# P·V of the banded attention with split operands, and a new order table, in a two-layer encoder trunk

## The chip, the cores and the metric

One core of a Trainium2 chip. The metric is the device time of one execution in microseconds (us), less is better. The kernel before takes 986.03 us, the median of three runs (985.98 to 986.37).

## The reference, cut to what matters

Two layers of an encoder on 256 tokens of width 1024. In each, three mixers read the same x (differential attention, a gated delta net in two directions, and attention in a band of 128 tokens to either side), their outputs are merged by gates, projected and normalised; a gated MLP with a short convolution follows. The change touches the third mixer, eight query heads on two key heads of 64:

```python
def window_gqa(q, k, v, sink, bias_table):
    ...
    s = jnp.where(valid[None, :, None, None], s + bias[None, None], -jnp.inf)
    sink_f = sink.astype(jnp.float32).reshape(G, R)[None, None, :, :, None, None]
    m = jnp.maximum(jnp.max(s, axis=-1, keepdims=True), sink_f)
    e = jnp.exp(s - m)
    p = e / (jnp.sum(e, axis=-1, keepdims=True) + jnp.exp(sink_f - m))
    o = jnp.einsum('bngrqk,bnkgd->bnqgrd', p.astype(vw.dtype), vw)
    return o.reshape(B, T, Hq * dh)

def reference(...):
    for l in range(DEPTH):
        h = hybrid_mixer(x, ...)
        x = layer_norm(DEEPNORM_ALPHA * x + h, ln1_g[l], ln1_b[l])
        f = conv_glu_ffn(x, ffn_up[l], ffn_conv[l], ffn_conv_b[l], ffn_down[l])
        x = layer_norm(DEEPNORM_ALPHA * x + f, ln2_g[l], ln2_b[l])
    return x
```

## The kernel before, in words

All arithmetic is float32 or near it. Most matmuls get there by a split: an operand is copied into a rounded type (`F32R`), the part named `hi`, and its remainder is subtracted from the original, `lo`; `mm3` then adds hi·hi, hi·lo and lo·hi, three matmuls of the rounded type. Weights come through SP's queue into `raw` tiles, ACT makes `hi` and DVE makes `lo` (`hi_take`, `lo_take`, and `hi_proj_tok`, `lo_proj_tok` for the projections `wo` and `fd`). Some smaller products are left in plain float32. `A.copy` may go to ACT or to DVE, whichever the plan chooses; `V` is DVE, `TE` is TensorE (PE).

The stages of a layer: products of x with the weights (`mm_proj_ch`, `mm_token_major`), the three mixers, branch products and gates (`mm_product`, labels `wb` and `gz`), the projection `wo` and a norm, eleven FFN chunks c = 0 to 10 (`mm_wide`), and the projection `fd` (`mm_run`, `ch_run`) with the second norm. The first two chunks of the FFN get their second factor from a token-major product (`s_token_major`), transposed on PE.

The program is not issued in the order in which it is written. Every operation is recorded with a cost, then ranked by the longest chain behind it, to which come a term for urgent pieces and the table `PRIO`, which holds a number for the label under which an operation was recorded (`plan.label`, as `(0, 'c', 2)` for layer 0, window attention, t = 2). Operations are placed on the engines by that rank. So one number in the table can move instructions on all engines. Names in `buf("tag")` draw from as many SBUF buffers as the tag has (`aT` 2, `q` 6, `vt` 2, `sv` 1, `o` 2), in program order; a tile waits until the tile before it in its buffer is done with. PSUM tiles of the mixers come from pools named `at`, `ch` and `mm`. All instructions pass through one helper, so the profile puts every one of them on line L195, and one finds them by the names of their tiles.

`window` runs four steps t; in each, two groups g (one per key head) multiply q and k into scores, add a bias, take the softmax, and transpose the probabilities into PSUM (`pt`, the rows `at_window<-tri,e_window`). They are copied to `aT`. Then P·V: 4 float32 matmuls, for each of two key blocks and each group, with 64 columns of v (`sv_window`) as the stationary operand and 256 queries moving; group 0 writes the lower and group 1 the upper 64 partitions of `po`. PE runs a float32 matmul as two passes, so the trace holds 64 passes for 32 matmuls. From `po` the rounded part and the remainder of the result are made, `yc`, which the branch product `wb` of this mixer reads.

## Time and profile before

| | us |
|---|---|
| median of three runs (985.98, 986.37, 986.03) | 986.03 |
| the profiled execution | 985.31 |
| its span, first to last instruction | 983.6 |
| PE busy | 961.5 |
| DVE busy | 759.4 |
| ACT busy | 605.8 |

TensorE's granted clock is 0.998 over the span. The busy time of PE is that of matmuls which overlap: the duration of one is longer than the distance to the next start, so prices of matmuls are read from start to start. A wait is the idle time of an engine ahead of an instruction, put down to the instruction of another engine that ended last. Rows of the timeline join instructions of one kind that follow each other (x6: six of them).

### The profile page before, as it was taken

The page shows a single profiled execution, that of the slowest core. Times are in us where ns is not written, and L with a number is a line of the kernel's source. Part 1 is how long each engine was busy: PE and PEld are TensorE (multiplying, and loading weights), DVE is VectorE, ACT ScalarE, POOL GpSimd, SP SyncE. Part 2 cuts the span into 40 slices and gives each one's busy share as a digit, 9 for nine tenths or more (in the row PEclk, how much of TensorE's full clock was granted, in tenths as well). Part 3 has the DMA queues.
Part 4 walks back from the last instruction along what each step waited for, and adds up shares of the span by engine and source line. Part 5 has one row for each costly group of instructions (what it writes and reads, how often), then busy time and mean ns, then how long its engine had stood idle before and what let it go on. Part 6 is the DMA issues. An engine that isn't in the chain of part 4 may idle for free.

```text
span 983.6 us, 16368 instructions
## 1 busy us (share of the span) xinstructions
PE 961.5 (98%) x6126; PEld 829.6 (84%) x6126; DVE 759.4 (77%) x1404; ACT 605.8 (62%) x1134; POOL 75.1 (8%) x84
## 2 busy tenths in 40 slices
PE   7999999999999999999999999999999999999996
PEld 6889899878888888878889998998778778888885
DVE  6799797666599988875689989866565988888655
ACT  5778757774465766653558777756744646666441
POOL 0510020000000100000005200100000010000000
PEclk9999999999999999999999999999999999999999
DMA  7554435355685766656635444334556665666661
GB/s 266 151 170 133 126 135 187 92 157 164 192 268 164 211 193 191 192 153 192 213 92 168 159 144 131 117 107 131 174 167 200 220 193 185 179 189 191 192 192 43
DMA packets 50100, 165.27 MB, mean 168 GB/s; under 512 B 5751, under 2 KB 11271, under 8 KB 50020
## 3 DMA queue, kind: packets, MB, share of 16 engines
q1 hardware_dynamic: 48644, 159.78, 52.3%
q0 software_dynamic: 1376, 4.43, 1.5%
q8 instruction: 48, 0.79, 0.3%
q14 instruction: 32, 0.26, 0.1%
HBM read 163.12 MB, written 1.07 MB: 167 GB/s over the span
## 4 chain that ended last, share of the span: by engine, by line
PE 83%; DVE 5%; ACT 4%; DMA 3%; issue 2%; POOL 2%; SPq 0%; POOLq 0%; ACTq 0%; DVEq 0%
PE mm_wide L195 23%; PE mm_product L195 19%; PE mm_proj_ch L195 15%; PE mm_run L195 7%; PE ch_run L195 6%; PE mm_token_major L195 3%; PE at_window L195 3%; PE ch_solve L195 2%; PE at_attention L195 2%; DMA raw_take<-in_w_dram 1%; ACT hi_take L195 1%; PE ch_gdn L195 1%; PE ch_finish L195 1%; PE ch_scan L195 1%; DVE lo_take L195 1%
## 5 line engine op out<-in xcount | busy, mean ns | idle before, releaser
L195 DVE TENSOR_TENSOR lo_take<-raw_take,hi_take 128x1024 fp32r<-128x1024 f32 x219 | 269.5, 1236 | 96.1 <-ACT hi_take L195 93.3
L195 ACT ACTIVATE hi_take<-raw_take 128x1024 fp32r<-128x1024 f32 x213 | 224.3, 1057 | 178.9 <-PE mm_wide L195 59.3
L195 PE MATMUL mm_wide<-xT,hi_take 128*128 128x512 f32 x640 | 224.0, 394 | 0.1
L195 PE MATMUL mm_proj_ch<-xT,hi_take 128*128 128x256 f32 x928 | 177.8, 287 | 1.1 <-ACT hi_take L195 1.1
L195 PE MATMUL mm_wide<-xT,lo_take 128*128 128x256 f32 x640 | 178.3, 283 | 0.0
L195 PEld LDWEIGHTS mm_proj_ch<-xT,hi_take 128*128 128x128 f32 x928 | 144.7, 189 | 4.2 <-ACT hi_take L195 1.7
L195 PEld LDWEIGHTS mm_wide<-xT,hi_take 128*128 128x128 f32 x640 | 119.4, 188 | 26.6 <-DVE xT L195 0.3
L195 PE MATMUL mm_proj_ch<-xT,lo_take 128*128 128x256 f32 x464 | 133.4, 288 | 0.0
L195 PE MATMUL mm_product<-hi_take,xT 128*128 128x512 f32 x384 | 128.4, 403 | 0.0
L195 PEld LDWEIGHTS mm_wide<-xT,lo_take 128*128 128x128 f32 x640 | 120.4, 188 | 1.4
L195 DVE TENSOR_TENSOR lo_proj_tok<-raw_proj_tok,hi_proj_tok 128x1024 fp32r<-128x1024 f32 x50 | 61.2, 1224 | 46.0 <-ACT hi_proj_tok L195 45.9
L195 ACT ACTIVATE hi_proj_tok<-raw_proj_tok 128x1024 fp32r<-128x1024 f32 x50 | 53.0, 1060 | 63.8 <-PE mm_run L195 35.0
L195 PEld LDWEIGHTS mm_proj_ch<-xT,lo_take 128*128 128x128 f32 x464 | 87.6, 189 | 2.7 <-DVE lo_take L195 1.1
L195 PEld LDWEIGHTS mm_product<-hi_take,xT 128*128 128x128 f32 x384 | 71.5, 189 | 15.4 <-issue 1.5
L195 PE MATMUL mm_product<-lo_take,xT 128*128 128x512 f32 x192 | 77.2, 402 | 0.0
L195 PEld LDWEIGHTS mm_product<-lo_take,xT 128*128 128x128 f32 x192 | 36.3, 189 | 6.8 <-DVE lo_take L195 0.2
L195 DVE SCALAR_TENSOR_TENSOR z_conv_silu<-mm_proj_ch,col_params,z_conv_silu 128x254 f32<-128x254 f32 (+1 forms) x96 | 39.4, 473 | 0.2
L195 POOL TENSOR_TENSOR s_tail<-s_tail,nhalf 128x1 f32<-128x1 f32 x8 | 8.2, 1023 | 383.4 <-DVE s_tail L195 383.4
L195 ACT ACTIVATE e_window<-e_window,s_window 128x256 f32<-128x256 f32 x54 | 25.7, 499 | 12.2 <-DVE s_window L195 12.1
L195 PEld LDWEIGHTS <-h_solve 128*128 128x128 f16 x640 | 25.6, 98 | 7.8 <-issue 3.4
L195 PE MATMUL mm_run<-hi_proj_tok,tile_encoder_trunk 128*128 128x512 f32 x88 | 27.5, 392 | 2.4 <-DVE tile_encoder_trunk L195 1.4
L195 PE MATMUL mm_run<-hi_proj_tok,ile_encoder_trunk 128*128 128x512 f32 x88 | 27.3, 390 | 0.0
(354 smaller groups left out, 1771.6 us busy)
## 6 DMA issues: line engine op xcount, KB each, us to landing
raw_take<-in_w_dram SPq DMA_DIRECT2D x226, 512.0 KB, 3.7
raw_proj_tok<-in_w_dram SPq DMA_DIRECT2D x60, 512.0 KB, 3.6
G_load_G<-band SPq DMA_DIRECT2D x24, 192.0 KB, 3.3
ya_ln_params<-in_lnp_dram POOLq DMA_DIRECT2D x16, 256.0 KB, 5.4
x<-in_xT_dram SPq DMA_DIRECT2D x4, 256.0 KB, 4.3
x<-in_x_dram SPq DMA_DIRECT2D x2, 512.0 KB, 4.5
out_dram<-x SPq DMA_DIRECT2D x8, 128.0 KB, 1.7
_tile_encoder_trunk<-in_w_dram SPq DMA_DIRECT2D x4, 128.0 KB, 5.1
```

Source lines behind the costliest of these rows:

```text
L195: op.ways.append((eng, lambda fn=fn, args=args, kw=kw: fn(*args, **kw), _cost(eng, name, outs, ins, args, kw), table))
```

## The change

1. v: in place of one copy to `sv`, v is rounded and its remainder is taken, and for each key block and group the two lie side by side (64 + 64 columns) in a tile of tag `vt`, which the gated delta net uses too.
2. The probabilities of each group are split: `ah` is the rounded copy (tag `aT`), `al` the remainder, by one DVE subtraction from PSUM (tag `q`).
3. P·V: for each group and key block `ah` and `al` are moved past the same 128 stationary columns; 8 matmuls for each t, all of the rounded type. The lower 64 partitions of `po` get the product with the rounded v, the upper 64 that with its remainder, one group beside the other.
4. The two halves are joined: two copies of 64x256 bring the upper half to SBUF (`y`, tag `o`), two DVE sums add the lower half. The rounded part and the remainder of the result are then made from SBUF in place of PSUM.
5. Labels are set in the projections, the FFN chunks and around the end of the norms, and the table `PRIO` is replaced by another with 168 entries in place of 95. The order on all engines changes.

```diff
-PRIO = {(0, 'a', 'ak', 0): 2.2, ...
+PRIO = {(0, 'a', 'aq', 0): -1.9, ...
@@ in proj_tok
         for n, (half, b) in enumerate(order):
+            plan.label = (l, nme, half, b)
...
+        plan.label = (l, nme, "tail", 0)
         norm.tail(0)
+        plan.label = (l, nme, "kept")
...
+        plan.label = (l, nme, "tail", 1)
         norm.tail(1)
+        plan.label = None
@@ in window
-        vt = buf("sv", (P, 2, P))
-        A.copy(vt, pv)
+
+        vt = buf("vt", (P, 2, 2, 2, 64), F32R)
+        pv = pv.rearrange("p t (g d) -> p t g d", g=2)
+        for tt in range(2):
+            A.copy(vt[:, tt, :, 0], pv[:, tt])
+            V.tensor_tensor(vt[:, tt, :, 1], pv[:, tt], vt[:, tt, :, 0].bitcast(F32), op=ALU.subtract)
...
-                aT = buf("aT", (P, 2, T))
-                A.copy(aT, pt)
-                aTs.append(aT)
-            po = ps_at((P, T))
-            for kb in range(2):
-                for g in range(2):
-                    TE.matmul(po[g * 64:(g + 1) * 64], vt[:, kb, g * 64:(g + 1) * 64], aTs[g][:, kb], start=kb == 0, stop=kb == 1)
-            hs, ls, po = blocks(yh[t // 2][:, t % 2]), blocks(yl[t // 2][:, t % 2]), flip(po)
-            A.copy(hs, po)
-            V.tensor_tensor(ls, po, hs.bitcast(F32), op=ALU.subtract)
+                ah, al = buf("aT", (P, 2, T), F32R), buf("q", (P, 2, T), F32R)
+                A.copy(ah, pt)
+                V.tensor_tensor(al, pt, ah.bitcast(F32), op=ALU.subtract)
+                aTs.append((ah, al))
+            po = ps_at((P, 2, T))
+            for g in range(2):
+                for kb in range(2):
+                    for n, a_ in enumerate(aTs[g]):
+                        TE.matmul(po[:, g], vt[:, kb, g].rearrange("p a b -> p (a b)"), a_[:, kb], start=kb == n == 0, stop=kb == n == 1)
+            y = buf("o", (P, T))
+            for g, r in enumerate(rows):
+                A.copy(y[r], po[rows[1], g])
+            for g, r in enumerate(rows):
+                V.tensor_tensor(y[r], po[rows[0], g], y[r], op=ALU.add)
+            hs, ls, y = blocks(yh[t // 2][:, t % 2]), blocks(yl[t // 2][:, t % 2]), flip(y)
+            A.copy(hs, y)
+            V.tensor_tensor(ls, y, hs.bitcast(F32), op=ALU.subtract)
@@ in the layer loop
         if norms:
+            plan.label = (l, "x", 2)
             norms.pop().finish()
+            plan.label = None
...
+        plan.label = (l, "ft")
         ft = token_major("ft", l, "s")
         for c in range(NFF // 2):
+            plan.label = (l, "f", c)
...
             if c == 2:
+                plan.label = (l, "x", 1)
                 norms.pop().finish()
+        plan.label = None
```

How the order changes at three places. A row is an instruction: operation, output tile, input tiles, size of the output; x2 stands for two alike. The numbers behind a name tell its tiles apart and differ between the two kernels.

PE at the first P·V of layer 0 (t = 0), before; `sv_window` is v, `aT_window` the probabilities, `mm_proj_ch` a product of x with weights:

```order
L195 MATMUL mm_product_5_486<-hi_take_40_492,ya_attention_1_324 128x512
L195 MATMUL mm_proj_ch_15_494<-xT,hi_take_41_496 128x256 x2
L195 MATMUL at_window_1_524<-aT_window_1_517,sv_window_1_507 64x256
L195 MATMUL at_window_1_524<-aT_window_2_523,sv_window_1_507 64x256
L195 MATMUL at_window_1_524<-aT_window_1_517,sv_window_1_507 64x256
L195 MATMUL mm_proj_ch_15_494<-xT,lo_take_41_497 128x256
L195 MATMUL mm_proj_ch_15_494<-xT,hi_take_41_496 128x256 x2
```

and now, with `vt_window` the rounded v and its remainder, `aT_window` and `q_window` the two parts of the probabilities, and products of another stage around it:

```order
L195 MATMUL mm_product_9_584<-hi_take_46_590,xT 128x512
L195 MATMUL at_window_1_526<-aT_window_1_517,vt_window_1_507 128x256
L195 MATMUL at_window_1_526<-q_window_1_518,vt_window_1_507 128x256
L195 MATMUL at_window_1_526<-aT_window_1_517,vt_window_1_507 128x256
L195 MATMUL at_window_1_526<-q_window_1_518,vt_window_1_507 128x256
L195 MATMUL at_window_1_526<-aT_window_2_524,vt_window_1_507 128x256
L195 MATMUL at_window_1_526<-q_window_2_525,vt_window_1_507 128x256
L195 MATMUL at_window_3_532<-tri,e_window_3_530 128x128 x4
L195 MATMUL at_window_1_526<-aT_window_2_524,vt_window_1_507 128x256
L195 MATMUL at_window_1_526<-q_window_2_525,vt_window_1_507 128x256
L195 MATMUL mm_product_9_584<-hi_take_46_590,xT 128x512
```

Four float32 matmuls of 64 columns have become eight of 128, with the transposes of another t among them.

PE at the entry of `fd` in layer 0, before: the last matmuls of the last FFN chunk's `mm_wide`, eight transposes of `s_token_major` for chunks 0 and 1, and the first `mm_run`:

```order
L195 MATMUL mm_wide_40_969<-xT,hi_take_109_971 128x512
L195 MATMUL mm_wide_40_969<-xT,lo_take_109_972 128x256
L195 MATMUL mm_tile_encoder_trunk_1_770<-tri,s_token_major_1_757 128x128
L195 MATMUL mm_tile_encoder_trunk_1_770<-tri,s_token_major_2_759 128x128
L195 MATMUL mm_tile_encoder_trunk_1_770<-tri,s_token_major_1_757 128x128
L195 MATMUL mm_tile_encoder_trunk_1_770<-tri,s_token_major_2_759 128x128
L195 MATMUL mm_tile_encoder_trunk_2_783<-tri,s_token_major_1_757 128x128
L195 MATMUL mm_tile_encoder_trunk_2_783<-tri,s_token_major_2_759 128x128
L195 MATMUL mm_tile_encoder_trunk_2_783<-tri,s_token_major_1_757 128x128
L195 MATMUL mm_tile_encoder_trunk_2_783<-tri,s_token_major_2_759 128x128
L195 MATMUL mm_run_3_984<-hi_proj_tok_6_982,z_tile_encoder_trunk_1_771 128x512
L195 MATMUL mm_run_3_984<-lo_proj_tok_6_983,z_tile_encoder_trunk_1_771 128x512
```

Now the transposes stand some 300 rows earlier, in the FFN, among the token-major product's last rows and `mm_wide_21`:

```order
L195 MATMUL mm_wide_21_883<-xT,lo_take_90_886 128x256
L195 MATMUL mm_wide_21_883<-xT,hi_take_90_885 128x512
L195 MATMUL mm_tile_encoder_trunk_1_782<-tri,s_token_major_2_771 128x128
L195 MATMUL mm_tile_encoder_trunk_1_782<-tri,s_token_major_1_769 128x128
L195 MATMUL mm_tile_encoder_trunk_1_782<-tri,s_token_major_2_771 128x128
L195 MATMUL mm_tile_encoder_trunk_2_795<-tri,s_token_major_2_771 128x128
L195 MATMUL mm_tile_encoder_trunk_2_795<-tri,s_token_major_1_769 128x128
L195 MATMUL mm_tile_encoder_trunk_2_795<-tri,s_token_major_2_771 128x128
L195 MATMUL mm_wide_21_883<-xT,lo_take_90_886 128x256
```

and the entry of `fd` has become:

```order
L195 MATMUL mm_wide_40_981<-xT,hi_take_109_983 128x512
L195 MATMUL mm_wide_40_981<-xT,lo_take_109_984 128x256
L195 MATMUL mm_run_3_996<-hi_proj_tok_6_994,z_tile_encoder_trunk_1_783 128x512
L195 MATMUL mm_run_3_996<-lo_proj_tok_6_995,z_tile_encoder_trunk_1_783 128x512
L195 MATMUL mm_run_3_996<-hi_proj_tok_6_994,z_tile_encoder_trunk_2_784 128x512
L195 MATMUL mm_run_3_996<-hi_proj_tok_6_994,z_tile_encoder_trunk_1_783 128x512
L195 MATMUL mm_run_3_996<-lo_proj_tok_6_995,z_tile_encoder_trunk_1_783 128x512
L195 MATMUL mm_run_3_996<-hi_proj_tok_6_994,z_tile_encoder_trunk_2_784 128x512
L195 MATMUL mm_run_4_997<-hi_proj_tok_6_994,z_tile_encoder_trunk_1_783 128x512
```

The transposes, and so the steps on DVE and ACT that follow them, have left the entry of `fd`; `mm_run_3` follows `mm_wide_40` directly.

SP's queue in the first 30 us, before (`raw_take` are weights, `yc_bias_table` the operand of the matmul that makes the bias table, `tb` its other operand):

```order
L195 DMA masks<-in_masks_dram 128x896
L195 DMA raw_take_3_147<-in_w_dram 128x1024
L195 DMA raw_take_4_150<-in_w_dram 128x1024
L195 DMA raw_take_5_161<-in_w_dram 128x1024
L195 DMA raw_take_6_164<-in_w_dram 128x1024
L195 DMA tb<-in_rel_bias_dram 32x12
L195 DMA raw_take_7_168<-in_w_dram 128x1024
L195 DMA raw_take_8_171<-in_w_dram 128x1024
L195 DMA raw_take_9_181<-in_w_dram 128x1024
L195 DMA yc_bias_table_1_97<-in_onehot_dram 33x512
L195 DMA raw_take_10_184<-in_w_dram 128x1024
L195 DMA band<-yc_bias_table_1_100 12x512
```

and now:

```order
L195 DMA masks<-in_masks_dram 128x896
L195 DMA sv_product_1_101<-in_wab_dram 128x128
L195 DMA tb<-in_rel_bias_dram 32x12
L195 DMA raw_take_3_147<-in_w_dram 128x1024
L195 DMA yc_bias_table_1_97<-in_onehot_dram 33x512
L195 DMA raw_take_4_150<-in_w_dram 128x1024
L195 DMA raw_take_5_161<-in_w_dram 128x1024
L195 DMA raw_take_6_164<-in_w_dram 128x1024
L195 DMA sv_product_2_1108<-in_wab_dram 128x128
L195 DMA raw_take_7_168<-in_w_dram 128x1024
L195 DMA band<-yc_bias_table_1_100 12x512
L195 DMA raw_take_8_171<-in_w_dram 128x1024
```

The operands of the bias table and the band made from it have moved up past weight loads, and two small loads (`sv_product`) lie among them. On PE the matmul `at_bias_table` moved from row 99 to row 51, to the 21st place behind the beginning of `mm_token_major`.

## Rows read from the trace of the kernel before

**Rows 1.** The page, busy time: engine, us (share of the span), instructions.

```profile
PE 961.5 (98%) x6126; PEld 829.6 (84%) x6126; DVE 759.4 (77%) x1404; ACT 605.8 (62%) x1134; POOL 75.1 (8%) x84
```

**Rows 2.** PE's waits: for what, us in total, times, longest us.

```profile
PE mm_proj_ch L195 <- ACT _tile_encoder_trunk L195: 5.9, 2, 4.9
PE mm_run L195 <- DVE tile_encoder_trunk L195: 1.4, 1, 1.4
PE mm_proj_ch L195 <- ACT hi_take L195: 1.1, 2, 0.8
PE mm_run L195 <- ACT tile_encoder_trunk L195: 1.0, 1, 1.0
...
PE at_window L195 <- DVE s_window L195: 0.3, 1, 0.3
...
PE at_window L195 <- DVE o_attention L195: 0.2, 1, 0.2
```

**Rows 3.** Busy time by stretches: length, then us busy (instructions) of each engine.

```profile
150.00:220.00 70.00, 69.47 (x492) 60.36 (x491) 47.18 (x131) 49.96 (x132) 4.51 (x4) 1.00 0.49 144
...
660.00:720.00 60.00, 60.00 (x334) 47.67 (x334) 37.28 (x95) 40.67 (x101) 2.01 (x2) 1.00 0.48 140
```

**Rows 4.** PE's groups by form: instructions | us busy, mean ns | idle before.

```profile
L195 PE MATMUL at_window<-aT_window,sv_window 128*64 128x256 f32 x64 | 12.8, 396 | 0.0
```

**Rows 5.** Timeline of PE at 182 us: start, us, instructions in a row.

```profile
181.81 1.08 PE L195 MATMUL at_window<-aT_window,sv_window 128*64 128x256 f32 x6
182.82 0.39 PE L195 MATMUL mm_proj_ch<-xT,lo_take 128*128 128x256 f32 x1
```

**Rows 6.** Timeline of PE at 665 us.

```profile
664.48 0.28 PE L195 MATMUL mm_proj_ch<-xT,hi_take 128*128 128x256 f32 x1
664.69 1.40 PE L195 MATMUL at_window<-aT_window,sv_window 128*64 128x256 f32 x8
666.02 0.39 PE L195 MATMUL mm_proj_ch<-xT,hi_take 128*128 128x256 f32 x1
666.24 0.28 PE L195 MATMUL mm_proj_ch<-xT,lo_take 128*128 128x256 f32 x1
```

**Rows 7.** Timeline of PE at 196 us.

```profile
195.57 0.63 PE L195 MATMUL at_window<-s_window,h_stacked 128*128 128x256 f32 x4
196.04 0.40 PE L195 MATMUL mm_proj_ch<-xT,hi_take 128*128 128x256 f32 x2
```

**Rows 8.** Timeline of PE at 430 us, the entry of fd in layer 0.

```profile
429.60 1.04 PE L195 MATMUL tile_encoder_trunk<-tri,s_token_major 128*128 128x128 f32 x8
431.64 0.50 PE L195 MATMUL mm_run<-hi_proj_tok,tile_encoder_trunk 128*128 128x512 f32 x1 [1.01 <-ACT tile_encoder_trunk L195]
...
434.25 0.73 PE L195 MATMUL mm_run<-hi_proj_tok,tile_encoder_trunk 128*128 128x512 f32 x2 [1.41 <-DVE tile_encoder_trunk L195]
```

**Rows 9.** DVE's groups by form from 150 to 220 us: columns as in Rows 4.

```profile
L195 DVE TENSOR_TENSOR N_decay<-ch_solved,beta_gdn_scalars 128x512 f32<-128x512 f32 x4 | 2.6, 680 | 1.3 <-PE ch_solved L195 1.3
...
L195 DVE TENSOR_TENSOR s_window<-mm_proj_ch,s_window 64x256 fp32r<-64x256 f32 x2 | 0.8, 422 | 0.4 <-ACT s_window L195 0.4
```

**Rows 10.** ACT's groups by form from 150 to 220 us.

```profile
L195 ACT ACTIVATE s_window<-mm_proj_ch 64x256 fp32r<-64x256 f32 x4 | 1.5, 374 | 0.0
```

**Rows 11.** Timeline of PE at 217 us, the last P·V of layer 0.

```profile
217.50 1.50 PE L195 MATMUL at_window<-aT_window,sv_window 128*64 128x256 f32 x8
```

**Rows 12.** Timeline of ACT at 219 us, the copy behind it.

```profile
219.03 0.39 ACT L195 ACTIVATE yc_window<-at_window 128x256 fp32r<-128x256 f32 x1 [1.17 <-PE at_window L195]
```

**Rows 13.** Timeline of PE at 15 us, the beginning of token_major.

```profile
15.51 0.39 PE L195 MATMUL mm_token_major<-hi_take,xT 128*128 128x512 f32 x1
15.74 0.39 PE L195 MATMUL mm_token_major<-lo_take,xT 128*128 128x512 f32 x1
```

**Rows 14.** Timeline of SP's issues at 12 us.

```profile
12.09 4.68 SPq L195 DMA_DIRECT2D raw_take<-in_w_dram  x4
```

**Rows 15.** The tile tb: its load from issue to landing.

```profile
DMA to landing us min/median/max: 5.9/5.9/5.9
```

**Rows 16.** Timeline of DVE at the end of the program.

```profile
979.03 0.42 DVE L195 TENSOR_TENSOR q_tail<-q_tail,ya_ln_params 128x256 f32<-128x256 f32 x1 [0.73 <-ACT q_tail L195]
```

More of the change, by code (lines that the diff above doesn't have):

```diff
@@ L48 @@
 WHOLE = ()
-PRIO = {(0, 'a', 'ak', 0): 2.2, (0, 'a', 'ak', 1): -4.9, (0, 'a', 'aq', 1): -2.6, (0, 'a', 0): 4.1, (0, 'a', 1): -5.5, (0, 'a', 2): 1.0, (0, 'a', 3): -2.7, (0, 'ab', 0): 4.3, (0, 'ak', 0): -2.5, (0, 'aq', 0): 1.1, (0, 'aq', 1): 1.1, (0, 'av', 0): 5.7, (0, 'c', 'ckv', 0): -8.6, (0, 'c', 'cq', 0): 1.8, (0, 'c', 'cq', 1): 9.5, (0, 'c', 0): -2.0, (0, 'c', 1): -1.0, (0, 'c', 2): -4.2, (0, 'c', 3): 4.2, (0, 'ckv', 0): -4.2, (0, 'cq', 0): 1.8, (0, 'cq', 1): 11.9, (0, 'finish'): 8.4, (0, 'gate', 0): -15.6, (0, 'gate', 1): -3.2, (0, 'gz', 1): -1.6, (0, 'gz', 3): 2.0, (0, 'gz', 4): -8.6, (0, 'gz', 5): -0.8, (0, 'k', 'gate', 0): 2.5, (0, 'k', 'k', 0): -7.3, (0, 'k', 'k', 1): -0.5, (0, 'k', 'q', 0): 1.6, (0, 'k', 'q', 1): -2.1, (0, 'k', 'v', 1): 0.3, (0, 'k', 0): -3.5, (0, 'k', 1): -5.6, (0, 'q', 1): 6.9, (0, 'scan'): -13.4, (0, 'v', 0): -0.8, (0, 'wb', 0): -7.9, (0, 'wb', 1): -20.3, (0, 'wb', 2): 9.2, (0, 'wb', 3): 0.9, (0, 'wb', 4): -5.6, (1, 'a', 'ak', 0): -4.0, (1, 'a', 'ak', 1): 6.5, (1, 'a', 'aq', 0): 5.4, (1, 'a', 'aq', 1): 3.6, (1, 'a', 3): 0.3, (1, 'ab', 0): -3.6, (1, 'ak', 0): 0.4, (1, 'ak', 1): 6.6, (1, 'aq', 1): -0.3, (1, 'c', 0): 6.5, (1, 'c', 1): 0.8, (1, 'c', 3): -10.4, (1, 'ckv', 0): -4.2, (1, 'cq', 0): 7.6, (1, 'cq', 1): -10.9, (1, 'finish'): 6.3, (1, 'gate', 0): 2.0, (1, 'gate', 1): -2.8, (1, 'gz', 0): -2.9, (1, 'gz', 2): 2.1, (1, 'gz', 3): -3.6, (1, 'gz', 4): 1.2, (1, 'gz', 5): 12.7, (1, 'k', 'ab', 0): -3.9, (1, 'k', 'gate', 0): 9.3, (1, 'k', 'gate', 1): 6.1, (1, 'k', 'k', 0): 4.3, (1, 'k', 'q', 0): -5.8, (1, 'k', 'q', 1): -4.7, (1, 'k', 'v', 0): 5.9, (1, 'k', 'v', 1): -1.4, (1, 'k', 1): -5.3, (1, 'q', 0): 10.2, (1, 'q', 1): -4.3, (1, 'scan'): -5.9, (1, 'solve'): -3.9, (1, 'wb', 0): -10.8, (1, 'wb', 1): -23.6, (1, 'wb', 3): 6.8, (1, 'wb', 4): 4.9, (1, 'wb', 5): 13.3, (0, 'k', 'ab', 0): -1.4, (0, 'k', 'gate', 1): -0.1, (0, 'k', 'v', 0): 4.3, (0, 'q', 0): 0.2, (1, 'aq', 0): -3.6, (1, 'av', 0): -1.9, (1, 'gz', 1): 0.7, (1, 'v', 0): 4.6, (1, 'wb', 2): 4.1}
```

1 line of the change is left out of this document (added).

## The prediction

> **What bounds the kernel now.** I read first the shares of busy time. TensorE (PE) is busy in 98% of the span [rows 1], so a microsecond is worth something only if it is taken from PE's own row of instructions or from the waits in that row. The waits of PE come next [rows 2]: eleven groups, from 5.9 us (the start, before the first weights are there) down to 0.2 us, 12.8 us in all. Two of them, 1.4 and 1.0, stand at one place, the entry of `fd` in layer 0. Without these and the start 4.5 us are left, in pieces of at most 0.8. Only the start, this entry and PE's own work can therefore give back anything that a measurement sees (0.2%, or 2 us). DVE and ACT have room in the stretches in which window attention runs: of 70 and of 60 us PE fills 69.47 and 60.00, DVE 47.18 and 37.28, ACT 49.96 and 40.67 [rows 3]. The profiled execution took 985.31 us, 1.7 of them around the span of 983.6; the median of the runs shown is 986.03, 0.7 above it. The sum is made against 985.31 and the 0.7 is added at the end.
>
> **P·V on PE.** Before there are 4 float32 matmuls for each t. The trace holds 64 passes for the 32 of both layers, each with a stationary operand 64 wide [rows 4]. Their mean of 396 ns is not their price, because matmuls overlap; the price is the distance from start to start. Six passes take 182.82 - 181.81 = 1.01 us [rows 5], eight take 666.02 - 664.69 = 1.33 [rows 6]. The 64 passes lie in 13 such runs, of which these are two, and by the same reading the 13 add up to 11.9 us. To this comes the passage from one number format to the other: the matmul ahead of a run lasts 664.69 - 664.48 = 0.21 and the one after it 666.24 - 666.02 = 0.22 [rows 6], where the same form costs 0.12 among its like (below). That is 0.19 for one excursion into float32. After the change there are 64 single matmuls of rounded operands, 128x128 by 256 columns. Four of that form took 196.04 - 195.57 = 0.47, or 0.118 each [rows 7], so 64 take 7.55. The difference is 7.55 - 11.9 = -4.3. Counted through the order of the whole program PE goes from rounded operands to float32 119 times before and 107 times after, so 12 excursions of 0.19 go, another -2.3. **First term: -6.6.** Bounds: -4.3 if the excursions cost nothing on balance, -6.8 if all 13 runs save theirs. One reason is left for no gain at all here, and it is a rival below.
>
> **The entry of `fd` in layer 0.** Before, eight transposes of `s_token_major` stand directly ahead of the first `mm_run`. They begin at 429.60, the first `mm_run` waits 1.01 us for ACT and the second `mm_run` tile's next matmuls 1.41 us for DVE [rows 8], which still have to multiply, round and subtract what was just transposed. After, the transposes stand some 300 rows earlier, among `mm_token_major_4` and `mm_wide_21`, about 57 us of PE work ahead of `fd` (their matmuls at the distances above), and between the last `mm_wide_40` and the first `mm_run` there is nothing. The operands are made long before. The weights of the first `mm_run` are of the same kind as before, and twelve matmuls in a row use them. **Second term: -2.4** (1.01 + 1.41). What is late next is the remainder of those weights, which DVE makes after the remainder that `mm_wide_40` uses; that is 2.7 us of PE work later against 1.2 us for one such subtraction, so I put nothing against it. Bounds: 0 if a new wait of the same size stands there, -2.4.
>
> **What the probabilities and v cost on DVE and ACT.** For each group `al` is one DVE subtraction of 128x512 out of PSUM, as `N_decay<-ch_solved` at 680 ns [rows 9], 16 in all. For each t there are two ACT copies of 64x256 at 374 ns [rows 10] and two DVE sums of the same shape at 422 ns [rows 9]. `hs` and `ls` are made as before, now from SBUF. v is copied in two pieces with two subtractions, about 0.4 us each, twice in the program. Per layer DVE gets 8 x 0.68 + 8 x 0.42 + 0.8 = 9.6 us, ACT 8 x 0.37 + 0.4 = 3.4. In the stretches of [rows 3] DVE has 22.8 and 22.7 us without work, ACT 20.0 and 19.3. The load fits; what it costs is time between dependent steps. The Trainium skill, "TensorEngine Tiling (Array Packing)", section "Performance Considerations", says that once TensorE is made faster the copying out of PSUM may become what bounds. No row of the trace before shows that here; by that rule DVE's 9.6 us would stand on the path in each layer, and the sum would be 19 us higher than by the rows.
>
> **The end of the window chain.** Where is this on the path? After the last P·V of a layer `wb` multiplies the last y. Before, the steps follow each other almost without a gap: the last P·V ends at 217.50 + 1.50 = 219.00 [rows 11] and the copy on ACT begins at 219.03 and takes 0.39 [rows 12]. After, the chain to `hs` is two copies, two sums and a copy: 2 x 0.37 + 2 x 0.42 + 0.39 = 2.0, with 0.03 for each of five passages 2.1, and one more subtraction of 0.42 to `ls`. The order has 11 matmuls of 512 columns between the last P·V and the first product that reads this y, in either layer. At 15.74 - 15.51 = 0.23 each [rows 13] they last 2.5 us. So 0.4 us of cover is left over `hs` and about none over `ls`; if a weight's subtraction (1.2 us) stands ahead in DVE's queue, the product waits about 0.8. With two such places and a half chance: **third term +0.8**, bounds 0 and +4 (each of the eight t's by 0.5). The v tile now waits for a `vt` buffer that the scan of the gated delta net frees. In the new order the scan is done before window attention starts, so this costs nothing; if it were late, everything of P·V would shift behind PE work that is there anyway.
>
> **The rest of the order.** The new table moves work on all engines. At the start the matmul `at_bias_table` now stands 21 matmuls behind the beginning of `mm_token_major`, so PE reaches it at 15.51 + 21 x 0.23 = 20.3 [rows 13]. Its operand is loaded by an issue that moved up on SP past three weight loads: the four loads that began at 12.09 [rows 14] leave one ahead of it, so it is issued near 13.4, and if it takes the 5.9 us of the neighbouring small load [rows 15] it lands at 19.3. One microsecond of margin; everything on PE stands behind it if it is late, at 1 to 2 us. At the end of the program less PE work lies between the last two results of `fd` (counted in the order at these distances, 5.7 us against 8.2), so that some of the first half's last steps fall into DVE's idle 0.73 us at 979.03 [rows 16]: **+0.1**. Other waits: 4.5 us before, and I see neither a reason for fewer nor for more; 0, bounds -4.5 and +4.5.
>
> **Sum.** -6.6 - 2.4 + 0.8 + 0.1 = -8.1, so 985.31 - 8.1 = 977.2 for an execution like the profiled one, and 978 with the 0.7 to the median.
>
> **The rivals.** (1) *The gain is given back.* With 98% of PE's time filled, any order has to hide everything anew, and this one carries more work on DVE. If the other waits double (+4.5) and the window's chains cost their upper bound (+4 in place of 0.8), the sum is -0.4 - and 985.6; with half of it about 982. For it: the start has a margin of only a microsecond, and more than a thousand dependent steps on DVE stand in a new order. Against it: the waits before are small and scattered. (2) *Slower: the window's chain bounds.* Each t now has `al` (0.68), two copies (0.75) and two sums (0.84) more between transposes and y, with passages and queueing about 2.9 us. If PE had nothing to put in between, eight t's would cost 8 x 2.9 = 23, against -9 of gain: +14, about 1000. It decides from 9 / 8 = 1.1 us exposed in each t. For it: the chain is longer by itself, and the rule of the paragraph on DVE and ACT leans this way. Against: before, P·V does not appear among the waits of PE but for `at_window` with 0.3 us [rows 2], and the new order has products and other groups' transposes between. (3) *The change does not do what it says*: a matmul of rounded operands with 128 stationary columns costs what a float32 pass of 64 costs (11.9 / 64 = 0.186). Then the first term is -2.3 at most and the time 982 to 984. The four of [rows 7] are of exactly this form and stand against it. (4) *More is gained*: the other waits shrink too, to under 974.
>
> **How the numbers follow.** Forecast (974 to 982) 0.70; gain given back 0.14, of which a third still is faster by over 0.2% and most of the rest within; slower by the window's chain 0.08; no shorter P·V 0.03; more gained 0.05. The range leaves out the far ends of the last, of the slower case and of the first rival's upper part: 974 to 984.5. Faster than 984.0: 0.70 + 0.05 + 0.06 + 0.02 = 0.83; within 0.2%: 0.09; slower: 0.08.
>
> **What would show it.** In the profile after: `at_window` with 128x128 stationary operands, 64 of them in P·V with a distance of 0.12 us (first term); no wait of `mm_run` at the first entry of `fd` (second); waits of `mm_product` for `yc_window` under a microsecond (third); PE's busy time lower by about 6 us and the sum of its waits near 11. The forecast is wrong if waits of `at_window` for `q_window` or `o_window`, or new waits for weights in the FFN, add up to more than 6 us.

## The result and the profile after

The changed kernel takes 974.6 us (median of four runs, 972.8 to 975.9) against 986.2 before (985.98 to 986.98): ratio 0.9886, 95% interval 0.9873 to 0.9900, 11.6 us less. The forecast was 978.0 in a range from 974.0 to 984.5: the direction and the range were right, the gain was forecast at 8 us and is 11.6. The two profiled executions, 985.31 and 972.79 us, lie 12.5 apart; the terms below are measured between them.

On the page PE's busy time has fallen by 9.0 us against [rows 1] (about 6 was forecast), DVE's has risen by 18.1 and ACT's by 4.9:

```profile
PE 952.5 (98%) x6126; PEld 831.6 (86%) x6126; DVE 777.5 (80%) x1439; ACT 610.7 (63%) x1153; POOL 71.4 (7%) x84
```

The sum of PE's waits has fallen from 12.8 to 9.0 us (near 11 was forecast). These are all of them (engine, what waited, for what: us in total, times, longest); they answer to [rows 2]:

```profile
PE mm_proj_ch L195 <- ACT _tile_encoder_trunk L195: 5.2, 2, 4.9
PE mm_run L195 <- ACT kk_product L195: 1.4, 1, 1.4
PE mm_proj_ch L195 <- ACT hi_take L195: 1.1, 2, 0.8
PE mm_token_major L195 <- DVE xT L195: 0.5, 1, 0.5
PE mm_product L195 <- ACT hi_take L195: 0.3, 1, 0.3
PE at_window L195 <- DVE h_stacked L195: 0.3, 1, 0.3
PE ch_solve L195 <- ACT h_solve L195: 0.2, 1, 0.2
```

Both waits at the entry of `fd` are gone, the small ones have shrunk from 4.5 to 2.4 us, and one of 1.4 us is new, of `mm_run` for `kk_product`.

P·V after the change, the last of layer 1, in PE's timeline (start, us, instruction; five more of the eight matmuls stand in the place of the dots). It answers to [rows 5, 6]:

```profile
699.55 0.39 PE L195 MATMUL mm_product<-hi_take,yc_window 128*128 128x512 f32 x1
699.78 0.28 PE L195 MATMUL at_window<-aT_window,vt_window 128*128 128x256 f32 x1
699.89 0.28 PE L195 MATMUL at_window<-q_window,vt_window 128*128 128x256 f32 x1
...
700.61 0.28 PE L195 MATMUL at_window<-q_window,vt_window 128*128 128x256 f32 x1
```

The distance is 0.12 us from one matmul to the next, and the product ahead of them lasts 699.78 - 699.55 = 0.23, nothing more than among its like. All 64 take 8.21 us from start to start (11.90 before), and their neighbours lose 0.63 (3.15 before): 15.05 has become 8.84.

The entry of `fd` in layer 0, PE, which answers to [rows 8]:

```profile
425.62 0.28 PE L195 MATMUL mm_wide<-xT,lo_take 128*128 128x256 f32 x1
425.74 0.40 PE L195 MATMUL mm_run<-hi_proj_tok,tile_encoder_trunk 128*128 128x512 f32 x1
```

`mm_run` begins 0.12 us behind the last `mm_wide`; there is no gap.

### The profile page after: what moved, and what is told of

The parts are those of the page before. It is cut to its first block, busy times and chain, and to the rows that moved or that the text cites. A ratio compares the mean times of both kernels' runs of the same rounds, so it can differ in the third digit from the quotient of the medians.

```text
span 971.1 us, 16462 instructions
## 1 busy us (share of the span) xinstructions
PE 952.5 (98%) x6126; PEld 831.6 (86%) x6126; DVE 777.5 (80%) x1439; ACT 610.7 (63%) x1153; POOL 71.4 (7%) x84
## 4 chain that ended last, share of the span: by engine, by line
PE 86%; ACT 6%; DVE 4%; issue 2%; DMA 1%; POOL 1%; SPq 0%; POOLq 0%; ACTq 0%
PE mm_wide L195 23%; PE mm_product L195 17%; PE mm_proj_ch L195 14%; PE ch_run L195 8%; PE mm_run L195 8%; PE mm_token_major L195 4%; PE ch_solve L195 2%; ACT hi_take L195 2%; PE ch_gdn L195 2%; PE at_window L195 2%; PE at_attention L195 2%; PE ch_scan L195 1%; PE ch_finish L195 1%; DVE lo_take L195 1%; ACT e_window L195 1%
## 5 line engine op out<-in xcount | busy, mean ns | idle before, releaser
L195 ACT ACTIVATE hi_take<-raw_take 128x1024 fp32r<-128x1024 f32 x208 | 219.1, 1058 | 151.1 <-PE mm_product L195 45.1
L195 ACT ACTIVATE e_window<-e_window,s_window 128x256 f32<-128x256 f32 x62 | 28.9, 498 | 9.1 <-DVE s_window L195 8.9
```

Source lines behind the costliest of these rows:

```text
L195: op.ways.append((eng, lambda fn=fn, args=args, kw=kw: fn(*args, **kw), _cost(eng, name, outs, ins, args, kw), table))
```

## The experiments

All times are medians; the runs of before that were made beside them had medians of 985.3 (the first four kernels), 986.3 (the next four) and 985.2 (the last four), so kernels of different groups are compared by their ratios to before. 0.001 of a ratio is 1 us; two ratios are called different only where their intervals do not overlap.

| kernel | us | ratio to before, 95% interval |
|---|---|---|
| changed kernel again (e4) | 973.5 | 0.9880, 0.9866 to 0.9894 |
| old P·V, new table (e1) | 979.4 | 0.9943, 0.9931 to 0.9954 |
| new P·V, old table (e2) | 992.5 | 1.0074, 1.0062 to 1.0086 |
| before, layer 0's FFN numbers only (e3) | 991.4 | 1.0066, 1.0052 to 1.0079 |
| without the al matmuls (e7) | 973.4 | 0.9867, 0.9853 to 0.9881 |
| without al at all (e8) | 972.0 | 0.9855, 0.9838 to 0.9872 |
| without the joining sums (e9) | 973.8 | 0.9879, 0.9863 to 0.9895 |
| joining copies three times (e10) | 987.5 | 1.0013, 1.0003 to 1.0023 |
| new numbers for the mixers only (e5) | 983.5 | 0.9982, 0.9966 to 0.9998 |
| new numbers for FFN and projections only (e6) | 990.9 | 1.0057, 1.0042 to 1.0072 |
| a weight tile rounded later (e11) | 978.4 | 0.9930, 0.9915 to 0.9945 |
| the same, without al (e12) | 973.5 | 0.9883, 0.9865 to 0.9902 |

### Which half of the change gives the gain

**The changed kernel once more**, with no edit.

> The changed kernel itself once more, for the spread of its executions (972.8 to 975.9 so far) and for a second trace. Theory: the 1.6 us that the first 48 matmuls of the start lost between the traces is the landing of the first loads, which are issued alike in both, and changes from execution to execution; so times again spread over about 3 us and the first token_major matmul begins anywhere between 13.9 and 15.5. Rival (the start is faster by the new order): it begins at 13.9 again and the times lie within 1 us of 972.8.

Measured: 973.5 (973.0 to 974.2), so the spread was 1.2 us here, not 3: in this the theory missed, and the rival's 1 us about 972.8 did too. In its trace `mm_token_major` begins at 14.19, between the two; more on the start below.

**Old P·V under the new labels and table.** The edit takes the body of `window` from before:

```diff
-        vt = buf("vt", (P, 2, 2, 2, 64), F32R)
+        vt = buf("sv", (P, 2, P))
...
-            po = ps_at((P, 2, T))
+            po = ps_at((P, T))
```

> The changed kernel with the old P·V (float32, 64 columns, v in sv) under the new labels and table. Theory (two separate gains): the 6.2 us that P·V with its neighbours lost between the two traces (15.05 to 8.84) come back and the rest of the gain stays: 974.6 + 6.2 = about 981, and no wait of mm_run at the entry of fd in layer 0. Rival A (the new order is only good for the new P·V): 985 or more. Rival B (the order does nearly all): 975 to 977.

Measured: 979.4, 5.9 us under the before of the same runs. The theory's number nearly held: putting the old P·V back costs 5.8 us (979.38 - 973.54). There is no wait at the entry of `fd`. From the list of PE's waits, the longest after the start's:

```profile
PE ch_tail L195 <- DVE q_tail L195: 1.3, 1, 1.3
```

The parts are not quite those of the theory. From the first `mm_token_major` to the end of the last matmul PE works 949.3 us and waits 5.6; in the trace of the changed kernel again it is 944.2 and 4.6. And the 64 old passes take 10.6 us from start to start here, not the 11.9 of before, because more of them stand together and in pairs. PE, a whole run of eight, and a run of two with the product behind it:

```profile
685.47 1.08 PE L195 MATMUL at_window<-aT_window,sv_window 128*64 128x256 f32 x8
686.49 0.66 PE L195 MATMUL at_window<-tri,e_window 128*128 128x128 f32 x4
...
700.88 0.65 PE L195 MATMUL at_window<-aT_window,sv_window 128*64 128x256 f32 x2
701.46 0.49 PE L195 MATMUL mm_product<-hi_take,xT 128*128 128x512 f32 x1
```

Eight passes take 686.49 - 685.47 = 1.02 us, two alone 0.58: in the run of eight the passes begin in pairs, 0.006 to 0.007 us apart. So the price of the old P·V is in part one of the order. By an estimate from these rows, eight whole runs would take 8 x 1.02 = 8.2 us, and with 0.19 for each of eight passages into float32 and back, as the prediction has it, 9.7, against 8.84 for the new P·V with its neighbours. An order that keeps the old P·V whole is a rival way to most of that gain; no kernel here tries it.

**New P·V under the old table.**

```diff
-PRIO = {(0, 'a', 'aq', 0): -1.9, ...
+PRIO = {(0, 'a', 'ak', 0): 2.2, ...
```

> The changed kernel with the table of before; labels that the old table does not hold count as zero. Theory (two separate gains): 986.2 - 6.2 = 980, up to 981 with small waits at the end of the window chain; the two waits of mm_run at the entry of fd (2.4 us) are there as before. Rival A (the longer window chain bounds if the order is not made for it): 988 to 1000, with waits of at_window or mm_product for q_window, o_window or yc_window. Rival B (the order does nearly all): 985 to 986.

Measured: 992.5, 7.2 us *slower* than before and 18.9 slower than the changed kernel. The theory of two separate gains fell, and rival A came true. PE's waits from the first `mm_token_major` on come to 14.2 us (7.1 before), and 4.7 of the 7.1 more stand at one place, the last t of layer 1. PE at the last t of layer 1:

```profile
719.60 0.84 PE L195 MATMUL at_window<-tri,e_window 128*128 128x128 f32 x4 [1.93 <-ACT e_window L195]
...
722.45 0.42 PE L195 MATMUL at_window<-q_window,vt_window 128*128 128x256 f32 x1
725.05 0.80 PE L195 MATMUL mm_product<-hi_take,yc_window 128*128 128x512 f32 x1 [2.19 <-ACT yc_window L195]
725.64 0.63 PE L195 MATMUL mm_product<-lo_take,yc_window 128*128 128x512 f32 x1
726.07 1.06 PE L195 MATMUL mm_product<-hi_take,yc_window 128*128 128x512 f32 x2
```

the steps behind the last P·V on ACT:

```profile
722.90 0.77 ACT L195 ACTIVATE o_window<-at_window 64x256 f32<-64x256 f32 x2 [1.82 <-PE at_window L195]
724.58 0.42 ACT L195 ACTIVATE yc_window<-o_window 128x256 fp32r<-128x256 f32 x1 [0.91 <-DVE o_window L195]
```

and on DVE:

```profile
723.70 0.85 DVE L195 TENSOR_TENSOR o_window<-at_window,o_window 64x256 f32<-64x256 f32 x2 [1.90 <-ACT o_window L195]
```

This is the chain whose length the prediction worked out as 2.1 us: it begins with the end of P·V at 722.45 + 0.42 = 722.87, and the product starts at 725.05, 2.18 later, with nothing put in between. PE waits 2.19 us for it, 1.93 for the probabilities just before and 0.6 within P·V. Behind the wait the products are slow: from 725.64 to 726.07 one takes 0.43 us in place of 0.23. The granted clock tells why (stretch: length, busy us of the engines; the number after POOL's is the clock, 1.00 is 2.4 GHz, 0.50 is 1.2 GHz):

```profile
304.00:308.00 4.00, 3.04 (x10) 2.53 (x11) 2.72 (x10) 0.07 (x1) 0.67 (x1) 0.68 0.34 120
434.00:438.00 4.00, 2.82 (x7) 2.24 (x8) 2.33 (x4) 1.19 (x2) 0.00 (x0) 0.65 0.40 129
...
724.00:728.00 4.00, 2.95 (x7) 2.40 (x8) 0.96 (x3) 0.42 (x1) 0.00 (x0) 0.50 0.00 0
```

In the middle of these stretches the clock had fallen to its lower level, at three places, each behind a wait: the norm ahead of the FFN (304 us), the entry of `fd` in layer 0 (434), the end of the window chain (720). The matmuls in the three spells took about 1.6, 1.6 and 2.3 us longer than at the upper level, by their distances. The wait at the first place, 1.5 us, is new as well, and is not of the window chain. At the second place the waits are those of before, 1.0 and 1.4 us; in the trace of before the clock stayed up there:

```profile
432.00:436.00 4.00, 2.59 (x12) 1.81 (x11) 3.39 (x7) 1.23 (x2) 0.00 (x0) 1.00 0.46 144
```

So the same two waits cost 2.4 us or 4.0.

**The second term alone.** The kernel before, with the labels of the token-major product and of the FFN chunks, and of the new table layer 0's numbers for these:

```diff
...
+        plan.label = (l, "ft")
         ft = token_major("ft", l, "s")
         for c in range(NFF // 2):
+            plan.label = (l, "f", c)
```

> The kernel before with only the labels of the token-major product and the FFN chunks, and only layer 0's numbers for them from the new table; P·V and all other numbers are as before. The transposes of s_token_major move ahead of the FFN's middle. Theory: the stall at the entry of fd goes (2.4 us of waits, 3.0 from start to start), so 983 to 984. Rival (something else is late at the same place, or the moved work makes new waits in the FFN): 985.5 to 987.

Measured: 991.4, 6.1 us slower. The stall behind the transposes is gone, and the rival has come true in its place, beyond its 987:

```profile
PE mm_run L195 <- ACT tile_encoder_trunk L195: 3.8, 1, 3.8
PE mm_wide L195 <- DVE tile_encoder_trunk L195: 1.9, 1, 1.9
```

Both are new: `mm_run` now waits 3.8 us for the rounded result of the last FFN chunk, which the same numbers put right ahead of it, and `mm_wide` 1.9 for the halves to be summed. Behind the first the clock is at its lower level:

```profile
462.00:466.00 4.00, 3.13 (x7) 2.44 (x8) 0.85 (x2) 0.63 (x1) 0.00 (x0) 0.50 0.42 131
```

The numbers that end waits of 2.4 us in the changed kernel cost 6 where the rest of the table is not made for them. They move more than the transposes: nine of the ten are of FFN chunks.

**The table in two halves.** The new table holds 168 numbers. One kernel has only those of the mixers and their products, another the old ones there and the new ones for the projections, the FFN and the ends of the norms.

```diff
-PRIO = {(0, 'a', 'aq', 0): -1.9, ..., (1, 'x', 1): 3.8}
+PRIO = {(0, 'a', 'aq', 0): -1.9, ...}
```

> The changed kernel with the new table cut to the labels of the mixers and their products; the projections, the FFN and the ends of the norms have no numbers, as before the change. Theory (losses of the new P·V under the old table stand at single places, each with its own wait and a spell of half clock behind it): the waits at the end of the window chain in layer 1 are gone, the entry of fd in layer 0 costs 3 to 5 us again, so 977 to 980. Rival (the order is one whole, and half a table is as bad as the old one): 988 or more.

> The changed kernel with the old table's numbers for the mixers and the new table's for the projections, the FFN and the ends of the norms. Theory: the entry of fd in layer 0 is without a wait, the window chain of layer 1 waits as under the old table (some 8 us with the half clock) and layer 0's mixers are some 4 us longer than in the changed kernel, so 984 to 987. Rival: 990 or more, or below 977 if the mixers' numbers do not matter.

Measured: 983.5 and 990.9. The first lies between its theory and its rival, the second has missed its theory and lies where its first rival had it. By the ratios, from the new P·V under the old table the mixers' numbers bring 9.1 us and the others, on top of them, another 10.0; without them the others bring 1.7, which the intervals do not tell from nothing. With the mixers' numbers the end of the window chain is covered, and the waits at `fd` are there in both layers, which the first trace (of before) showed in layer 0 only:

```profile
PE mm_run L195 <- DVE tile_encoder_trunk L195: 1.4, 1, 1.4
PE mm_run L195 <- DVE ile_encoder_trunk L195: 1.4, 1, 1.4
PE mm_token_major L195 <- ACT xT L195: 1.3, 1, 1.3
```

With only the others, the window chain of layer 1 waits as under the old table (2.2 and 1.9), `fd` is free, and the norms wait three times:

```profile
PE mm_token_major L195 <- DVE xT L195: 3.6, 3, 1.7
PE mm_product L195 <- ACT yc_window L195: 2.2, 1, 2.2
PE at_window L195 <- ACT e_window L195: 1.9, 1, 1.9
```

The runs of the first of the two spread from 979.5 to 988.2, and the time goes with the mean granted clock: 0.998 in the run of 979.5, 0.996 at 981.9 to 982.7, 0.991 to 0.994 at 984.2 to 986.0 and 0.990 at 988.2. One kernel, one order, and 9 us between its executions. The one that was traced, 985.95, has three spells at the lower level, and by the distances of the matmuls in them they cost about 1.6 us each, 5 of the 6.4 us that it lies above the fastest. What the others waited for was not traced.

### What bounds the window stage after the change

The next four kernels keep the changed kernel's order: the plan is made with every operation, and then some are not issued, or issued more than once. In the first the 32 matmuls with `al` are left out (the remainder of the probabilities is missing from the result):

```diff
-                op.call()
+                if not op.skip:
+                    op.call()
...
                     for n, a_ in enumerate(aTs[g]):
+                        plan.skip = n == 1
```

> The changed kernel in exactly its own order, with the 32 matmuls of the probabilities' remainder (al) left out of P·V; al is still made on DVE. Theory (PE's row is the bound there, 0.118 us each): 32 x 0.118 = 3.8 us less, about 970. Rival (P·V is covered by waits for DVE and ACT around it): within 1 us of the changed kernel, 973 to 974.

Measured: ratio 0.9867 against 0.9880 for the whole kernel, about 1.3 us less with intervals that overlap, not 3.8. The rival is nearer. In the trace, from the first `mm_token_major` to the end of the last matmul, PE's work is 2.6 us shorter than in the changed kernel again (941.6 against 944.2) and its waits are 2.5 longer (7.2 against 4.6), so the stretch takes 948.8 us in both. All of PE's waits come to 11.8 us in place of 8.9. From the list:

```profile
PE mm_run L195 <- ACT kk_product L195: 1.9, 1, 1.9
...
PE mm_product L195 <- ACT hi_take L195: 0.8, 1, 0.8
...
PE at_window L195 <- DVE q_window L195: 0.5, 2, 0.3
...
PE at_window L195 <- DVE o_window L195: 0.4, 2, 0.3
PE mm_product L195 <- DVE yc_window L195: 0.3, 1, 0.3
```

`q_window`, `o_window` and `yc_window` are the steps of this very chain on DVE; they make 1.2 of the 2.9 us more. The wait for `kk_product` has grown by 0.7 (1.2 in the changed kernel again), the one for a weight (`hi_take`) by 0.5. PE was not the only bound: at these places the work on ACT and DVE is hardly shorter than PE's row.

The second leaves out the subtraction that makes `al`, too:

```diff
+                plan.skip = True
                 V.tensor_tensor(al, pt, ah.bitcast(F32), op=ALU.subtract)
```

> As the kernel without the al matmuls, same order, and the 16 subtractions that make al (0.69 us each on DVE, 11 us in all) left out too. Theory (DVE's extra work lies beside PE's): the same time as without the al matmuls, within 1 us. Rival (the subtractions stand on the path, as if copying out of PSUM bounded the stage): several us less, up to 11.

Measured: 0.9855, 1.2 us less than the one before it, with intervals that overlap. 11 us of DVE work bring about 1 us: most of it lies beside PE's, as the theory has it.

The third leaves out the 16 sums of the two halves, the fourth issues the 16 copies ahead of them three times each:

```diff
             for g, r in enumerate(rows):
+                plan.skip = True
                 V.tensor_tensor(y[r], po[rows[0], g], y[r], op=ALU.add)
```

```diff
+                plan.skip = 3
                 A.copy(y[r], po[rows[1], g])
...
-                op.call()
+                for _ in range(op.skip or 1):
+                    op.call()
```

> The changed kernel in exactly its own order, with the 16 DVE sums that join the two halves left out (the product with the rounded v is missing from the result), so that each t's chain is 0.85 us shorter. Theory (the chain is covered): within 0.5 us of the changed kernel, 973 to 974. Rival (the chain is on the path at some t): 0.85 us less for each t that is exposed, 1.7 for the two last ones, 6.8 for all eight.

> The changed kernel in exactly its own order, with the 16 copies that join the halves issued three times each, so that each t's chain is 1.5 us longer. Theory (only the last t of a layer has little cover, some 0.4 us): 2 x 1.1 = about 2 us more, 975 to 977, with waits of mm_product for yc_window. Rival A (every t is exposed): 8 x 1.5 = 12 more. Rival B (all covered): no change.

Measured: 0.9879 and 1.0013. A chain shorter by 0.85 us at each t changes nothing (0.9880 with it); a chain longer by 1.5 us costs 13 us, near 8 x 1.5. The third kernel went as the theory said, the fourth by its number as rival A. Its edit does two things: it lengthens the chain, and it gives ACT 11.5 us more to do (622.9 us busy against 611.4), which other stages share. Waits of the fourth, in its slowest execution (990.07; all of them 22.2 against 8.9):

```profile
PE at_window L195 <- DVE o_window L195: 4.7, 3, 1.7
PE mm_product L195 <- ACT yc_window L195: 3.7, 3, 1.3
```

These are 8.4 of the 13.3 us more; 1.7 are for a weight (`hi_take`, with a spell of the lower clock behind it) and 0.9 for `kk_product`. The larger part is not where the prediction looked, at the end of the chain: it is `at_window` that waits for the sums. Layer 1, on ACT the six copies:

```profile
690.60 2.42 ACT L195 ACTIVATE o_window<-at_window 64x256 f32<-64x256 f32 x6
```

the sums behind them on DVE:

```profile
693.05 0.85 DVE L195 TENSOR_TENSOR o_window<-at_window,o_window 64x256 f32<-64x256 f32 x2 [2.39 <-ACT o_window L195]
```

and PE's next scores, which are of another t:

```profile
694.05 0.72 PE L195 MATMUL at_window<-s_window,h_stacked 128*128 128x256 f32 x4 [1.71 <-DVE o_window L195]
```

They do not read what the sums make, but they need a PSUM tile of the pool `at`, which has two banks in the kernel, and the sums are the last to read one. So a t can be exposed through its tile, and not only the last one through its result: the six waits stand at 218.7, 694.1 and 701.7 us for a tile, at 225.4, 232.4 and 719.8 for a result. Not every t shows one. That a tile is what PE waits for is read from who released it; it was not tried with more tiles.

### The new wait in `wo` of layer 1

ACT ahead of the copy that PE waits 1.4 us for:

```profile
754.67 1.15 ACT L195 ACTIVATE D_weights<-raw_proj_tok 128x512 fp32r<-128x512 f32 x2 [2.70 <-DMA raw_proj_tok<-in_w_dram]
755.73 0.58 ACT L195 ACTIVATE kk_product<-at_product 128x512 fp32r<-128x512 f32 x1
```

`D_weights` rounds a weight tile, had waited 2.70 us for its load, and stood ahead of `kk_product` in ACT's queue. The edit is meant to put this rounding and its two subtractions right behind the two steps that make `kk_product`:

```diff
+        named = lambda op: op.outs[0].tensor.name
+        after = max(op.start for op in ops if named(op).startswith("kk_product") and named(op).endswith(("_5_1684", "_6_1685")))
+        for n, op in enumerate(o for o in sorted(ops, key=lambda o: o.start) if named(o).startswith("D_weights") and named(o).endswith(("_5_1714", "_6_1715", "_7_1716", "_8_1717"))):
+            op.start = after + 1e-6 * (n + 1)
         for op in sorted(ops, key=lambda o: o.start):
```

> The changed kernel in its own order but for four instructions: the rounding of one weight tile of wo in layer 1 (D_weights, two on ACT that wait for a load, and their two subtractions on DVE) now stands behind the copies of kk_product that PE waits for. Theory (that wait of 1.2 to 1.4 us is a load's, by way of ACT's queue): the wait of mm_run for kk_product falls below 0.3 and the time by about 1 us, to 972.5. Rival (kk_product is late by itself, or D_weights is now late): no change, 973 to 974.5.

Measured: 978.4, 0.5% *slower* than the changed kernel. The wait for `kk_product` is gone, as the theory has it, and a longer one has come:

```profile
PE ch_run L195 <- ACT hi_proj_tok L195: 2.4, 1, 2.4
```

ACT in this kernel:

```profile
755.47 0.60 ACT L195 ACTIVATE kk_product<-at_product 128x512 fp32r<-128x512 f32 x1 [2.16 <-PE at_product L195]
758.73 0.63 ACT L195 ACTIVATE N_weights<-raw_proj_tok 128x512 fp32r<-128x512 f32 x1 [2.67 <-DMA raw_proj_tok<-in_w_dram]
759.27 1.13 ACT L195 ACTIVATE D_weights<-raw_proj_tok 128x512 fp32r<-128x512 f32 x2
...
761.30 1.04 ACT L195 ACTIVATE hi_proj_tok<-raw_proj_tok 128x1024 fp32r<-128x1024 f32 x1
```

The next load's rounding (`N_weights`, 2.67 us of waiting) is now first, `D_weights` behind it, and `hi_proj_tok`, for which PE waits, begins at 761.30; in the changed kernel's trace its place was 758.83, in the second one 759.85. The loads are not late: that of `D_weights` landed at 755.89 and that of `N_weights` at 758.71, against 755.67 and 758.29 in the second trace. So the edit put `D_weights` behind a wait for a load that it does not need: its own had been there for 2.8 us, and all that stands behind it in ACT's queue came later. PE's wait became 2.4 us, with a spell of the lower clock behind it. Whether a rounding right behind `kk_product` would gain the 1 us is left open.

> As the kernel that rounds the weight tile later, and with the probabilities' remainder left out (no al on DVE, no al matmuls on PE; the result is less precise). Theory (the two gains are at different places and add up): 973.5 - 1 - 1.5 = 971. Rival (what one gives back the other already had, or another engine takes over): 972 to 973.5.

The last kernel joins this to the one without `al`; its edit is the two above. Ratio 0.9883, no better than the changed kernel (0.9880) and in the rival's range: the first edit was no gain, so there was nothing to add up. No kernel here is clearly faster than the changed one; without `al` it may be, by 0.25% with intervals that overlap, for a less precise product.

## Why the prediction was right, point by point

- **P·V, -6.6 forecast, -6.2 measured** (15.05 to 8.84). The matmuls gave 3.7, not 4.3, since some lie among transposes and 64 take 8.2, not 7.55; the neighbours gave 2.5 where 2.3 was worked out from the count of excursions. Two misses of opposite sign: the number is better than its parts. The prediction read 0.186 us a pass as the price of the old form, but runs of eight in the old P·V under the new table take 0.13 a pass, so part of the 3.7 is what the old order had cost. Whether the neighbours lost by the number format or by the 64 columns no run separates.
- **The entry of `fd`, -2.4 forecast, -2.4 of waits** and 0.6 more from start to start, as the transposes no longer end there. But the kernel with FFN numbers alone shows that the move is not worth this by itself.
- **The end of the window chain, +0.8 forecast, 0 measured**: no wait for `yc_window` in the trace after. Its length was right (2.1 forecast; 2.18 where it lay bare).
- **The end of the program, +0.1 forecast, 0.0 measured**: from the last matmul's end to the end of the span 9.1 us in both.
- **DVE and ACT, 19.2 and 6.8 more to do forecast, 18.1 and 4.9 measured**, and no wait for the new steps: it lies beside PE's work, as said.
- **Other waits, 0 forecast, about -2 measured, and +1.4.** The small waits of 4.5 us are 2.4, and the one of `kk_product` is new. This is the term that was mis-sized, within its bounds of 4.5; I had no row that spoke for either sign.
- **The start.** `at_bias_table` came in time. The first `mm_token_major` began at 13.92 (15.51 in [rows 13]), though the loads ahead of it are issued alike:

```profile
13.92 0.40 PE L195 MATMUL mm_token_major<-hi_take,xT 128*128 128x512 f32 x1
```

In the second trace of the changed kernel it began at 14.19, and the first 48 matmuls took between 8.5 and 10.7 us in the fourteen traces of this case, between 8.6 and 10.3 in the eight with the changed kernel's order up to there. One order alone shows as much between its executions, so the 1.6 of the 12.5 us between the two profiled ones cannot be put down to the change.

The sum of the terms is -6.2 - 3.0 - 2.1 + 1.4 = -9.9, with the start -11.5; 1.0 us is spread over pieces below 0.3, which no term had. So the gain came out larger than the forecast by small terms that went the right way, the start among them; only P·V and `fd` were foreseen.

**What was wrong in the reasoning, though the number held.** The prediction added the new order's worth to P·V's, as if either could be had alone. The runs say -5.9 us for the order with the old P·V, +7.2 for the new P·V with the old order, and -11.8 for both: the new P·V saves 6 us in an order that covers its longer chain, and the kernel is 7 us slower in one that does not. About 7.0 us of that loss stand at the end of the chain (4.7 of waits, 2.3 of slower matmuls), another 4.7 at the norm and at `fd`, and what P·V saves comes off again. The rival "slower: the window's chain bounds" named a mechanism that two kernels show, the old table's and the one with longer copies (8.4 us of waits for `o_window` and `yc_window`). Its chance of 0.08 rested on the order of the changed kernel, which was in view, and that was the reason to hold it low. The Trainium skill, "TensorEngine Tiling (Array Packing)", section "Performance Considerations", says of tiling that after a fourfold speedup of TensorE the copy out of PSUM may become the bottleneck. The speedup here is far smaller (P·V's rows from 11.9 to 8.2 us), and the traces show the beginning of it: without the al matmuls PE waited 0.9 us for `q_window` and `o_window`, which read PSUM and for which it had not waited before, and with the longer copies 5.1.

## What to carry to other kernels

An engine that is busy 98% of the time can still stand next to a chain of nearly its own length: taking 32 matmuls out brought about 1 us, no more than the noise, and adding 12 us beside them cost 13. Look for the chain through what it holds, not only through what it makes: by the traces here, the step that reads a PSUM tile last can decide when the next matmul may start. Before an operand's form is changed to make a matmul cheaper, look at whether the order splits the old ones up: eight old passes took 1.02 us together and two took 0.58. And a change to one stage and the order table are one change: half a table, a few of its numbers, or four instructions moved by hand left the kernel 5 to 19 us slower than the whole.

## What the runs showed of the hardware

A gap in PE's row can cost more than its length. Behind waits of 1 to 4 us the granted clock stood at 0.50 (1.2 GHz) in the traces of e2, e3, e5, e6, e10, e11 and e12, and by their distances the matmuls in such a spell lost about 1.5 to 3.3 us on top. Other waits of this size left it at 1.00: 1.4 us in the changed kernel, 1.7 and 1.6 in e10. With two waits of 1.0 and 1.4 us near each other it fell in e2 and in e5 and did not in the trace of before. In the runs of e5 the mean clock, from 0.998 to 0.990, goes with the time, from 979.5 to 988.2. A spread of executions under one kernel that is larger than its neighbours' can therefore be a sign of such waits. The gain of the change itself owes nothing to the clock: it is 0.998 over the span in both profiled executions.
